# Second layer's modulation inside the first U stage, one-hots over fewer groups, and gathers shared out anew

## The chip, the cores and the metric

One core of a Trainium2 chip runs the whole program. The time is the device time of one execution in microseconds (us); the kernel before was timed in three runs. Engines: TensorE (PE, with its weight loads PEld), VectorE (DVE), ScalarE (ACT), GpSimd (POOL) and SyncE (SP), which here only issues DMAs. Each engine has one queue that it works off in order.

## The reference, cut to what matters

Two layers work on 512 latent and 256 context tokens of width 1024. Each layer begins with a modulation, six vectors of 1024 for the latent stream and six for the context:

```python
mod   = (silu_c  @ w_mod[l] + b_mod[l])[:, None, :]
mod_c =  silu_cc @ w_mod[l] + b_mod[l]
sh1, sc1, g1, sh2, sc2, g2 = jnp.split(mod, N_MOD, axis=-1)
h_lat = rms_norm(x_lat, norm_mix[l]) * (1.0 + sc1) + sh1
```

Then come a mixer (windowed attention A, neighbourhood attention B, an RWKV-7 scan C, an output projection) and PEER: a retrieval in which 8 heads pick 16 of 16384 experts for each token, by product keys.

```python
q = (hb @ wq).reshape(PEER_CHUNK, PEER_HEADS, 2, PEER_QDIM // 2)
s = jnp.einsum('thpd,hpnd->thpn', q, sub_keys).astype(jnp.float32)
sv, si = lax.top_k(s, PEER_TOPK)
...
gate = jax.nn.softmax(best, axis=-1)
ue = jnp.take(u, expert, axis=0)
ve = jnp.take(v, expert, axis=0)
act = jax.nn.gelu(jnp.einsum('td,thkd->thk', hb, ue).astype(jnp.float32), approximate=False)
return jnp.einsum('thk,thkd->td', (gate * act).astype(hb.dtype), ve)
```

The modulation of a layer does not depend on the tokens. In the second layer the context needs no PEER.

## The kernel before, in words

`run` goes through the two layers, each as `project` (norm and input projection), `mix` (scan, attention, output projection) and `peer`. Matrix products with float32 accuracy are three products of halves: each operand is split into H (a cast on ACT) and L (a subtraction, mostly on DVE), and `mm3` (L132) issues H·H, H·L and L·H.

**Modulation.** `mod_unit` (L151) computes one of six units of a layer: eight loads of 128 x 1024 weights (`wmod`, 512 KB each, on SP's queue, L164), 32 products in four column groups of PE (L161), four for the bias, a copy on ACT (L170), two stores to memory (`mscr`, ACT's queue), and for shift and scale two transposes and a copy to columns (L177 to L184). The first layer's six units run in its `project`. Of the second layer's, the first two (`NM1`) run between the softmaxes of the first layer's attention (`fill`, L577), the other four in the second layer's `project`, at a lower priority than the norms (L257).

**Attention.** `soft` (L581) takes one softmax of 128 rows: maximum on DVE, exponential on ACT, sum and reciprocal on DVE, a scaling of up to 640 columns on DVE (L603), transposes on PE, a copy on ACT. There are 48 in the first layer and 32 in the second.

**PEER, dense.** The dense tokens (512 in the first layer, 384 in the second) go against all experts. `scores` (L1103) makes 16 blocks of key scores (per block wH on ACT, wL on DVE at L1120, 24 matmuls, top-16 on DVE); it runs for the context, the first layer's latents and the second layer's. The U stage runs over 32 groups of four blocks of 128 experts: a U row of two blocks is loaded, split into uH and uL (L1311, L1313), multiplied (`pa`), put through Gelu on ACT (L1317) and stored. In between run the units of `gated`: for each of the four dense token tiles (three in the second layer) a choice of experts on DVE, then four units that build the gate matrix W of 32 tokens from one-hots (`oh`, `og` on DVE, small f16 matmuls `pw`, a copy on ACT into W, a store to `wscr`). `GSPREAD` says over how many groups these units are spread. When they are all issued, their memory is closed and a pool `ar2` opens in its place, in which the last `LATE` blocks of Gelu outputs stay instead of being stored; the first such block belongs to group 24 in the first layer. The V stage then runs over the groups: G = Gelu output times W, split, and multiplied with the split V rows into eight accumulators (`py`).

**PEER, gathered.** The remaining tokens (256 of the context in the first layer, 128 latents in the second) are done by gathers (`Gather`): one indirect DMA on POOL's queue fetches, for 128 tokens, one expert's row of 8 KB (U and V), DVE multiplies the U half with the token (L1464) and adds the weighted V half to `accc` (L1470); 256 gathers in the first layer, 128 in the second. They are issued by `tick`: `NTICK` has, per layer, how many gathers a tick is worth: in the scores, in the first `NFIRST` groups of U, in the rest of U, and in V. A tick comes every second block. What is left after V goes out in `flush`. Two gathers (`NQ`) are accumulated together.

**The ring.** All large weights of these stages and all gathers share one ring of six rows (`gat.row`, `NROW`), 8 KB in each partition, 1 MB a row. A row is filled anew when the last reader of its sixth predecessor is done, in the order of the program.

**The order.** The kernel is written with a framework that orders the instructions of each engine ahead of time, by a simulated timeline and priorities; the order on the chip is then fixed. `high_priority(offset=...)` moves work forward or, negative, back; gathers get the strongest push.

Of the kernel before, what the change touches and what calls it, by code (L numbers as in the profile page):

```python
# [8 lines left out]
F32 = mybir.dt.float32  # L9
# [5 lines left out]
OP = mybir.AluOpType  # L15
# [3 lines left out]
P = 128  # L19
# [16 lines left out]
NROW = 6  # L36
NQ = 2
MOFF = 500
GSPREAD = (24, 20)
LATE = (28, 28)  # L40
NM1 = 2
NMW = (6, 4)
NRAW = 4
TC0 = 6
NPSC, NPSL = 2, 4
# [9 lines left out]
NPRT = 4  # L55
NQKB = {"qs": 3, "kh": 3, "kl": 2}

NTICK = ((1, 1.0, 1.5, 2.4), (0, 0, 1.06, 1.06))
NFIRST = (12, 3)
FEATS = (12, 13, 4, 0, 5, 1, 6, 2, 7, 3, 14, 8, 9, 10, 11)  # L60
LAT = (0, 1, 2, 3)
# [5 lines left out]
class Kernel:  # L67
    nw = 0

    def __init__(self, ctx, tc, i, out, dbg):  # L70
        self.ctx, self.tc, self.nc, self.i, self.out, self.dbg = ctx, tc, tc.nc, i, out, dbg
        self.cp = ctx.enter_context(self.pool(name="cp", bufs=1))
        self.mods = list(range(NM1))

        self.xsb = {}
        self.consts()
        self.scratch()
# [70 lines left out]
        for ch in chunks:  # L148
            self.mod_unit(l, ch, pool, ps, "pm")

    def mod_unit(self, l, ch, pool, ps, tag):  # L151

        nc, i = self.nc, self.i
        c = slice(ch * 1024, ch * 1024 + 1024)
        src = i["w_mod"][l, :, c].rearrange("(k p) n -> p k n", p=P)
        b = pool.tile([P, 256], F32, name="bmod", bufs=1)
        nc.sync.dma_start(b[0::32], i["b_mod"][l, c].rearrange("(j m) -> j m", j=4))
        pm = ps.tile([P, 512], F32, name=tag)

        def add(j, lhs, rhs, first, last):  # L160
            nc.tensor.matmul(pm[32 * j:32 * j + 32, 0:256], lhs, rhs, start=first, stop=last)  # L161
        for k in range(KC):
            w = pool.tile([P, 1024], F32, name="wmod")
            nc.sync.dma_start(w, src[:, k])  # L164
            for j in range(4):
                add(j, self.cs[:, k], w[:, j * 256:j * 256 + 256], k == 0, False)
        for j in range(4):
            add(j, self.cs[32 * j:32 * j + 1, KC], b[32 * j:32 * j + 1], False, True)
        r = pool.tile([P, 256], F32, name="rmod", bufs=1)
        nc.scalar.copy(r, pm[:, 0:256])  # L170
        for z in range(2):
            nc.scalar.dma_start(self.mscr[l][z, c].rearrange("(j m) -> j m", j=4), r[z::32])
        which, part = divmod(ch, 3)
        if part < 2:
            pt = ps.tile([P, 512], F32, name=tag)
            for h in range(2):
                nc.tensor.transpose(pt[:, h * P:h * P + P], r[:, h * P:h * P + P], self.ident)  # L177
            m = self.mcol[:, l, which, :, part]
            nc.vector.tensor_copy(m.rearrange("p z (j h) -> p z j h", h=2),
                                  pt[:, 0:256].rearrange("p (h j m) -> p m j h", h=2, j=4)[:, 0:2])  # L180
            if part:
                o = (NMIX, NFFN)[which]
                for z in range(2):
                    nc.vector.scalar_tensor_tensor(m[:, z], m[:, z], 1.0, self.colp[l][:, o:o + 8], OP.add, OP.mult)  # L184
# [43 lines left out]
    def project(self, l, st):  # L228
# [3 lines left out]
        hp_ = st.enter_context(self.pool(name="hp", bufs=1))  # L232
        hH = hp_.tile([P, KC, T], F32R, name="hH")
        hL = hp_.tile([P, KC, T], F32R, name="hL")
        def mods(chunks):
            if s3.pools is None:
                s3.pools = [s3.enter_context(self.pool(name="mp", bufs=NMW[l], side="right")),
                            s3.enter_context(self.pool(name="mps", bufs=2, space=PSUM, side="right"))]
            self.mod(l, chunks, *s3.pools)

        def src(t):
            if l == 0:
                return i["x"][t * P:(t + 1) * P] if t < 4 else i["ctx"][(t - 4) * P:(t - 3) * P]
            return self.xp[t * P:(t + 1) * P]
        with ExitStack() as s3:
            s3.pools = None
            if l == 0:
                mods(range(2))
            with ExitStack() as s2:
                np_ = s2.enter_context(self.pool(name="np", bufs=2))  # L250
                nps = s2.enter_context(self.pool(name="nps", bufs=2, space=PSUM))
                mc = self.mcol[:, l, 0]
                for tiles in (CTX, LAT[:2], LAT[2:]):
                    self.norm_T(src, mc, hH, hL, tiles, np_, nps)
            if l:
                self.gat.close()
            with self.tc.high_priority(offset=-MOFF):  # L257
                mods(range(NM1 if l else 2, 6))
        ps = st.enter_context(self.pool(name="pps", bufs=2, space=PSUM))
        psn = st.enter_context(self.pool(name="psn", bufs=2, space=PSUM, side="right"))  # L260
        xp_ = st.enter_context(self.pool(name="xp", bufs=1, side="right"))
# [302 lines left out]
    def attention(self, l, st):  # L564
# [7 lines left out]
        nc.sync.dma_start(sink, i["a_sink"][l].partition_broadcast(P))  # L572
        am = ap.tile([P, 2, P], F32, name="am")
        nc.sync.dma_start(am, i["amask"])
        mp = st.enter_context(self.pool(name="mp", bufs=2))

        def fill():  # L577
            if self.mods:
                self.mod_unit(1, self.mods.pop(0), mp, psl, "pl")

        def soft(parts, h, use_sink):  # L581

# [17 lines left out]
                nc.vector.tensor_tensor(m[:, 3:4], m[:, 3:4], m[:, 5:6], OP.add)  # L600
            nc.vector.reciprocal(m[:, 3:4], m[:, 3:4])
            n = sum(n for _, n in parts)
            nc.vector.tensor_scalar(pr[:, :n], pr[:, :n], m[:, 3:4], None, OP.mult)  # L603
            prT = a2.tile([P, 640], F32, name="prT", bufs=NPRT)
            c = 0
            for pl, n in parts:
# [38 lines left out]
        def heads_A(tiles, lat):  # L645
            k0_ = 0 if lat else NLAT
            q0 = tiles[0] * P
            for e in range(2):
# [3 lines left out]
                for a, t in enumerate(tiles):  # L652
# [6 lines left out]
                    for z in range(2):  # L659
                        pl = psl.tile([P, 512], F32, name="pl")  # L660
                        parts = [(pl, nk + 256)] if nk <= 256 else [(pl, nk), (psl.tile([P, 512], F32, name="pl"), 256)]
                        pc, n = parts[-1]
                        q = qs[z][:, a * P:(a + 1) * P]
                        qk_mm(pc[:, n - 256:n], q, hd, lambda x: x[:, NLAT - k0_:])
                        if lat:
                            qk_mm(pl[:, 0:nk], q, hd, lambda x: x[:, k0 * P:(k1 + 1) * P])
                            if k0 < t:
                                nc.vector.tensor_tensor(pl[:, 0:P], pl[:, 0:P], am[:, 0], OP.add)
                            if k1 > t:
                                nc.vector.tensor_tensor(pl[:, nk - P:nk], pl[:, nk - P:nk], am[:, 1], OP.add)  # L670
                        fill()
                        prTs.append(soft(parts, 2 * e + z, True))
                    weigh(pl, prTs, [vals] * 2, o[:, a * P:(a + 1) * P])
                keep(e, o, q0)
# [30 lines left out]
        for c in range(2):  # L705
# [3 lines left out]
            for j in range(4):  # L709
                prTs = []  # L710
                for z in range(2):
# [9 lines left out]
                          lambda x: x[:, :NLAT].rearrange("p (r w) -> p r w", w=64)[:, :, reg[j]:reg[j] + 32])  # L721
                    qk_mm(pl[:, 256:512], qb, hd[z], lambda x: x[:, NLAT:])
                    nc.vector.tensor_tensor(pl[:, 0:256], pl[:, 0:256], bias, OP.add)
                    fill()
                    prTs.append(soft([(pl, 512)], h, False))
                weigh(pl, prTs, [[vb[:, j, y, h * 64:h * 64 + 64] for y in range(2)] +
                                 [vc[:, y, h * 64:h * 64 + 64] for y in range(2)] for h in (2 * c, 2 * c + 1)],
# [375 lines left out]
    def scores(self, l, hH, hL, tiles, sv, sif, st, tick=None, side=None):  # L1103
# [6 lines left out]
        for c in range(16):  # L1110
# [6 lines left out]
            wH = sp2.tile([P, KC, P], F32R, name="wH")  # L1117
            nc.scalar.copy(wH, wr)
            wL = sp2.tile([P, KC, P], F32R, name="wL")
            nc.vector.tensor_tensor(wL, wr, wH.bitcast(F32), OP.subtract)  # L1120
            n = len(tiles)
            pq = psq.tile([P, n * P], F32, name="pq")
            for k in range(KC):
# [142 lines left out]
    def peer(self, l, st):  # L1266
# [11 lines left out]
        with ExitStack() as sb:  # L1278
# [15 lines left out]
            it = self.places(sp)  # L1294
            up = sb.enter_context(self.pool(name="up", bufs=2))
            psu = sb.enter_context(self.pool(name="psu", bufs=2, space=PSUM))
            pw = sb.enter_context(self.pool(name="pw", bufs=2, space=PSUM))

            def scored(g, late=None):
# [33 lines left out]
            for g in range(32):  # L1333
# [3 lines left out]
                if done == 5 * len(dense) and units:  # L1337
                    units = None
                    sg.close()
                    late = sr.enter_context(self.pool(name="ar2", bufs=1, side="right"))  # L1340
                scored(g, late)
        with ExitStack() as sb:
            vp = sb.enter_context(self.pool(name="vp", bufs=2))
            psv = sb.enter_context(self.pool(name="psv", bufs=1, space=PSUM))
# [76 lines left out]
class Gather:  # L1421
# [26 lines left out]
    def row(self):  # L1448
        return self.gp.tile([P, 2 * D], F32, name="row", bufs=NROW)
# [104 lines left out]
```

## Time and profile before

| what | value |
|---|---|
| median of three runs | 5100.42 us (5089.33 to 5117.75) |
| profiled execution | 5089.21 us |
| its span, first to last instruction | 5087.4 us |
| busy: PE, DVE, ACT, POOL | 87%, 73%, 34%, 26% |
| mean granted clock of TensorE | 0.906 of full |
| moved by DMA | 1186.55 MB, mean 233 GB/s |
| first layer: U stage, V stage | 1122 to 2057 us, 2057 to 2860 us |
| second layer: from 2870 us; U stage, V stage | 3830 to 4510 us, 4510 to 5060 us |

A busy PE is one with matmuls in flight; their ends are modelled, so matmuls overlap in the rows. The times of the stages are read from the first and last instructions of their lines. What an engine waited for is inferred from semaphore events. An engine's idle time matters only where that engine's work ends last.

### The profile page before, as it was taken

How to read it: one execution, taken by the hardware profiler on the slowest of the kernel's cores; microseconds unless marked ns; L12 is line 12 of the kernel's file. 1: busy time of each engine (PE TensorE's matmuls, PEld its weight loads, DVE VectorE, ACT ScalarE, POOL GpSimd, SP SyncE). 2: the span in 40 equal slices, each digit the busy share in tenths (PEclk: the TensorE clock that was granted, in tenths of full speed). 3: DMA queues.
4: the chain of work that ended last, by engine and by line, in shares of the span. 5: the costliest groups of instructions: out<-in, count | busy, mean ns of one | idle time of the engine just before them, and what ended most of it. 6: DMA issues, size and time to landing. Idle time of an engine off the chain costs nothing. (4 is left out here: it accounts for less than half of the span.)

```text
span 5087.4 us, 74067 instructions
## 1 busy us (share of the span) xinstructions
PE 4438.3 (87%) x27525; PEld 3679.1 (72%) x27525; DVE 3738.1 (73%) x7611; ACT 1731.5 (34%) x2881; POOL 1338.2 (26%) x1403
## 2 busy tenths in 40 slices
PE   7778797689999979898889596799698998988999
PEld 4558666567888867787777364687578997977887
DVE  3964658869967754798888867758589877556887
ACT  3433234333333322222222244324333443332333
POOL 0536632011111111232222235455011111112121
PEclk9779887799999989999999787779799998999999
DMA  7434665235777755899999942573424887567998
GB/s 273 134 104 125 190 203 177 90 128 197 250 260 283 281 217 214 305 372 371 367 364 368 349 162 87 131 204 111 157 100 170 305 296 278 215 236 256 342 357 299
DMA packets 573865, 1186.55 MB, mean 233 GB/s; under 512 B 63152, under 2 KB 376384, under 8 KB 520768
## 3 DMA queue, kind: packets, MB, share of 16 engines
q1 hardware_dynamic: 507072, 758.39, 44.8%
q0 software_dynamic: 61440, 418.41, 22.1%
q10 hardware_dynamic: 4992, 5.02, 0.3%
q8 instruction: 216, 3.54, 0.3%
q14 instruction: 145, 1.19, 0.1%
HBM read 1005.19 MB, written 176.50 MB: 232 GB/s over the span
## 5 line engine op out<-in xcount | busy, mean ns | idle before, releaser
L1453 POOL DMA_INDIRECT row<-in_uv,eidx x384 | 580.2, 1511 | 2465.2 <-DVE accc L1470 1369.1
L136 PE MATMUL pa<-hH,uL 128*128 128x512 f32 (+1 forms) x2048 | 757.9, 370 | 36.0 <-DVE uL L1313 35.9
L134 PE MATMUL pa<-hH,uH 128*128 128x512 f32 (+1 forms) x2048 | 754.5, 368 | 25.8 <-ACT ar L1317 21.6
L135 PE MATMUL pa<-hL,uH 128*128 128x512 f32 (+1 forms) x2048 | 752.4, 367 | 0.0
L135 PE MATMUL py<-vL,GH 128*128 128x512 f32 x1792 | 705.9, 394 | 26.6 <-DVE vL L1365 26.5
L136 PE MATMUL py<-vH,GL 128*128 128x512 f32 x1792 | 698.4, 391 | 0.0
L134 PE MATMUL py<-vH,GH 128*128 128x512 f32 x1792 | 625.2, 397 | 67.5 <-ACT vH L1363 44.1
L1464 DVE SCALAR_TENSOR_TENSOR row<-row,h2c 128x1024 f32<-128x1024 f32 x384 | 467.6, 1220 | 293.6 <-DMA row<-in_uv,eidx 293.3
L1470 DVE SCALAR_TENSOR_TENSOR accc<-row,dt,accc 128x1024 f32<-128x1024 f32 x384 | 491.6, 1280 | 5.4
L1311 ACT CAST uH<-row 128x1024 fp32r<-128x1024 f32 x256 | 268.5, 1050 | 653.7 <-PE pa L135 582.2
L136 PEld LDWEIGHTS pa<-hH,uL 128*128 128x128 f32 x2048 | 391.4, 191 | 84.8 <-DVE uL L1313 45.8
L134 PEld LDWEIGHTS py<-vH,GH 128*128 128x128 f32 x1792 | 340.9, 191 | 148.6 <-ACT vH L1363 53.4
L134 PEld LDWEIGHTS pa<-hH,uH 128*128 128x128 f32 x2048 | 391.6, 191 | 66.6 <-ACT ar L1317 22.2
L135 PEld LDWEIGHTS pa<-hL,uH 128*128 128x128 f32 x2048 | 390.9, 191 | 39.4
L135 PEld LDWEIGHTS py<-vL,GH 128*128 128x128 f32 x1792 | 341.3, 190 | 105.6 <-DVE vL L1365 34.5
L1313 DVE TENSOR_TENSOR uL<-row,uH 128x1024 fp32r<-128x1024 f32 x256 | 311.8, 1220 | 128.4 <-ACT uH L1311 127.5
L136 PEld LDWEIGHTS py<-vH,GL 128*128 128x128 f32 x1792 | 339.6, 189 | 70.7
L1370 ACT CAST GH<-G 128x512 fp32r<-128x512 f32 (+1 forms) x256 | 145.0, 567 | 637.7 <-PE py L135 414.9
L1365 DVE TENSOR_TENSOR vL<-row,vH 128x1024 fp32r<-128x1024 f32 x256 | 309.4, 1218 | 26.5 <-ACT vH L1363 26.5
L1363 ACT CAST vH<-row 128x1024 fp32r<-128x1024 f32 x256 | 262.5, 1043 | 41.7 <-DMA row<-in_uv 23.1
L1239 PE MATMUL pw<-og,oh 128*128 128x128 f16 x1792 | 237.7, 297 | 33.5 <-DVE og L1234 23.5
L1231 DVE TENSOR_TENSOR oh<-iota,ix 128x512 f16<-128x512 f16 x448 | 170.5, 419 | 104.8 <-PE pw L1239 103.9
(385 smaller groups left out, 8577.1 us busy)
## 6 DMA issues: line engine op xcount, KB each, us to landing
row<-in_uT SPq DMA_DIRECT2D x128, 1024.0 KB
row<-in_uv SPq DMA_DIRECT2D x128, 1024.0 KB
wscr<-W SPq DMA_DIRECT2D x28, 2048.0 KB
wmod<-in_w_mod SPq DMA_DIRECT2D x96, 512.0 KB
wt<-wscr SPq DMA_DIRECT2D x32, 1024.0 KB
row<-in_wq SPq DMA_DIRECT2D x24, 1024.0 KB
ascr<-aw SPq DMA_DIRECT2D x96, 256.0 KB
av<-ascr SPq DMA_DIRECT2D x48, 512.0 KB
```

What stands on the lines that cost most here:

```text
L134: mm(out, lh, rh, start=first, stop=False)
L135: mm(out, lh, rl, start=False, stop=False)
L136: mm(out, ll, rh, start=False, stop=last)
L1231: nc.vector.tensor_tensor(oh[:, z], self.iota4, ix[:, z, tt].unsqueeze(1).to_broadcast([P, P, 4]), OP.is_equal)
L1239: nc.tensor.matmul(pw[:, q], oh[:, 1, :, q], og[:, z, :, q], start=z == 0, stop=z == 1)
L1311: nc.scalar.copy(uH, ur)
L1313: nc.vector.tensor_tensor(uL, ur, uH.bitcast(F32), OP.subtract)
L1363: nc.scalar.copy(vH, vr)
L1365: nc.vector.tensor_tensor(vL, vr, vH.bitcast(F32), OP.subtract)
L1453: self.K.nc.gpsimd.indirect_dma_start(out=r, out_offset=None, in_=self.K.i[f"uv{self.l}"], in_offset=bass.IndirectOffsetOnAxis(ap=self.idx ...
L1464: nc.vector.scalar_tensor_tensor(rows[z][:, 0:D], rows[z][:, 0:D], 1.0, self.h[:, a], OP.mult, OP.mult, accum_out=dt[:, z:z + 1])
L1470: nc.vector.scalar_tensor_tensor(acc, v, dt[:, z:z + 1], acc, OP.mult, OP.add)
```

## The change

Five things change, all in the order or the place of work; what is computed stays.

- All six units of the second layer's modulation run in the first layer's U stage, one after each of the groups 4, 9, 14, 19, 24 and 29. Their weights come through the ring, two slices of 512 KB to a row, four rows a unit. `fill` and the units in the second layer's `project` are gone, with their pools.
- `GSPREAD` goes from (24, 20) to (22, 18): the units of `gated` are spread over fewer groups.
- `NTICK` changes in both layers: more gathers in scores and U, fewer in V.
- `soft` scales on ACT.
- `scores` subtracts wL on POOL.

```diff
-GSPREAD = (24, 20)
+GSPREAD = (22, 18)
-NM1 = 2
-NMW = (6, 4)
-NTICK = ((1, 1.0, 1.5, 2.4), (0, 0, 1.06, 1.06))
+NTICK = ((2, 1.2, 2.0, 2.1), (0, 0, 1.2, 1.0))
...
-    def mod_unit(self, l, ch, pool, ps, tag):
+    def mod_unit(self, l, ch, pool, ps, tag, row=None):
...
-            w = pool.tile([P, 1024], F32, name="wmod")
-            nc.sync.dma_start(w, src[:, k])
+            if row is None:
+                w = pool.tile([P, 1024], F32, name="wmod")
+                nc.sync.dma_start(w, src[:, k])
+            else:
+                if k % 2 == 0:
+                    w2 = row().rearrange("p (k n) -> p k n", k=2)
+                    nc.sync.dma_start(w2, src[:, k:k + 2])
+                w = w2[:, k % 2]
...
-            if l == 0:
-                mods(range(2))
+            if wc:
+                mods = (s3.enter_context(self.pool(name="mp", bufs=6, side="right")),
+                        s3.enter_context(self.pool(name="mps", bufs=2, space=PSUM, side="right")))
+                self.mod(l, range(2), *mods)
...
-            with self.tc.high_priority(offset=-MOFF):
-                mods(range(NM1 if l else 2, 6))
+            if wc:
+                with self.tc.high_priority(offset=-MOFF):
+                    self.mod(l, range(2, 6), *mods)
...
-        def fill():
-            if self.mods:
-                self.mod_unit(1, self.mods.pop(0), mp, psl, "pl")
...
-            nc.vector.tensor_scalar(pr[:, :n], pr[:, :n], m[:, 3:4], None, OP.mult)
+            nc.scalar.activation(pr[:, :n], pr[:, :n], AF.Copy, scale=m[:, 3:4])
...
-            nc.vector.tensor_tensor(wL, wr, wH.bitcast(F32), OP.subtract)
+            nc.gpsimd.tensor_tensor(wL, wr, wH.bitcast(F32), OP.subtract)
...
+            if wc:
+                mu = (sb.enter_context(self.pool(name="mu", bufs=1)),
+                      sb.enter_context(self.pool(name="psm", bufs=1, space=PSUM)))
...
                 scored(g, late)
+                if wc and g % 5 == 4:
+                    self.mod_unit(1, g // 5, *mu, "pm", gat.row)
```

## Rows read from the trace of the kernel before

**Rows 1.** The page: busy time of the engines, and memory rate in 40 slices.

```profile
PE 4438.3 (87%) x27525; PEld 3679.1 (72%) x27525; DVE 3738.1 (73%) x7611; ACT 1731.5 (34%) x2881; POOL 1338.2 (26%) x1403
...
GB/s 273 134 104 125 190 203 177 90 128 197 250 260 283 281 217 214 305 372 371 367 364 368 349 162 87 131 204 111 157 100 170 305 296 278 215 236 256 342 357 299
```

**Rows 2.** Busy time in stretches: length; PE, PEld, DVE, ACT, POOL; clock; DMA share; GB/s.

```profile
860.00:1050.00 190.00, 147.37 (x881) 122.21 (x880) 144.85 (x598) 62.63 (x130) 9.74 (x32) 0.82 0.27 93
...
1122.00:2057.00 935.00, 888.18 (x4378) 730.71 (x4377) 682.30 (x1579) 309.88 (x473) 145.57 (x137) 0.97 0.66 240
2057.00:2860.00 803.00, 717.54 (x3072) 582.50 (x3072) 695.40 (x944) 215.37 (x335) 242.27 (x162) 0.97 0.99 362
```

**Rows 3.** The same in shorter stretches at the end of the U stage.

```profile
1790.00:1830.00 40.00, 40.00 (x208) 33.24 (x207) 27.64 (x45) 14.70 (x23) 5.30 (x4) 1.00 0.76 286
1830.00:1870.00 40.00, 16.33 (x119) 12.88 (x117) 26.38 (x51) 9.63 (x17) 4.57 (x3) 0.56 0.62 231
...
1877.00:2057.00 180.00, 168.71 (x716) 137.28 (x714) 84.50 (x98) 46.39 (x69) 31.44 (x21) 0.96 0.52 190
```

**Rows 4.** Timeline of PE and ACT there: start, length, instruction [idle before <- releaser].

```profile
1874.68 0.80 PE L134 MATMUL pa<-hH,uH 128*128 128x512 f32 x1 [14.04 <-ACT ar L1317]
...
1874.04 1.09 ACT L1317 ACTIVATE ar<-pa 128x512 f32<-128x512 f32 x2 [12.76 <-DMA wscr<-W]
```

**Rows 5.** V stage, first layer: busy time; PE's longest wait (total us, times, longest).

```profile
2057.00:2840.00 783.00, 717.54 (x3072) 582.50 (x3072) 676.62 (x918) 214.55 (x331) 230.19 (x155) 0.98 0.99 361
...
PE py L134 <- ACT vH L1363: 44.1, 22, 5.3
```

**Rows 6.** Timeline of PE: the first work after the V stage.

```profile
2884.94 1.08 PE L161 MATMUL pm<-wmod,cs 128*32 128x256 f32 x8 [46.29 <-DMA wmod<-in_w_mod]
```

**Rows 7.** Groups by line: count | busy us, mean ns | idle before, releasers.

```profile
L1470 DVE SCALAR_TENSOR_TENSOR accc<-row,dt,accc 128x1024 f32<-128x1024 f32 x384 | 491.6, 1280 | 5.4
L1464 DVE SCALAR_TENSOR_TENSOR row<-row,h2c 128x1024 f32<-128x1024 f32 x384 | 467.6, 1220 | 293.6 <-DMA row<-in_uv,eidx 293.3
```

**Rows 8.** Timeline of PE: two groups of a modulation unit back to back.

```profile
2900.65 0.64 PE L161 MATMUL pm<-wmod,cs 128*32 128x256 f32 x8
2901.22 0.63 PE L161 MATMUL pm<-bmod,cs 1*32 1x256 f32 x8
```

**Rows 9.** Stretches, line 161 alone: length, PE busy, PEld busy, clock, DMA share, GB/s.

```profile
620.00:700.00 80.00, 12.99 (x144) 3.22 (x144) 0.96 0.75 223
2860.00:2920.00 60.00, 13.04 (x128) 2.95 (x128) 0.61 0.93 337
2920.00:3020.00 100.00, 15.36 (x160) 4.30 (x160) 0.89 0.56 192
```

**Rows 10.** PE's waits in the second layer's U stage.

```profile
PE pa L134 <- ACT ar L1317: 7.5, 1, 7.5
```

**Rows 11.** Groups by line: scaling, exponential, wL on DVE, wL on POOL.

```profile
L594 ACT ACTIVATE pr<-pl,sm 128x512 f32<-128x512 f32 (+2 forms) x96 | 57.2, 599 | 63.7 <-DVE sm L590 58.8 <-PE pg L859 2.1 <-DVE sm L600 1.3
...
L1120 DVE TENSOR_TENSOR wL<-row,wH 128x1024 fp32r<-128x1024 f32 x48 | 58.2, 1218 | 24.2 <-ACT wH L1118 20.3 <-PE pS L1129 3.8
...
L603 DVE TENSOR_SCALAR pr<-pr,sm 128x512 f32<-128x512 f32 (+2 forms) x80 | 45.8, 577 | 1.1
...
L224 POOL TENSOR_TENSOR wL<-wr,wH 128x1024 fp32r<-128x1024 f32 x10 | 25.6, 2562 | 133.3 <-ACT wH L223 75.8 <-DMA wr<-in_w_in 54.4 <-issue 3.1
```

**Rows 12.** PE's waits from 720 to 1000 us.

```profile
PE pl L608 <- DVE pr L603: 28.5, 8, 13.8
```

**Rows 13.** Timeline of POOL and DVE in the second layer's norm.

```profile
2912.73 2.35 POOL L224 TENSOR_TENSOR wL<-wr,wH 128x1024 fp32r<-128x1024 f32 x1 [54.35 <-DMA wr<-in_w_in]
...
2911.26 0.29 DVE L216 CAST hH<-f 128x256 fp32r<-128x256 f32 x1 [1.74 <-ACT f L212]
...
2913.15 2.18 DVE L216 CAST hH<-f 128x256 fp32r<-128x256 f32 x1 [1.14 <-ACT f L212]
```

**Rows 14.** SP's waits in the first layer's U stage, for U rows.

```profile
SPq L1304 <- DVE uL L1313: 76.6, 16, 27.8
...
SPq L1304 <- DMA row<-in_uv,eidx: 46.0, 5, 16.1
```

More of the change, by code (lines that the diff above doesn't have):

```diff
@@ L72, in __init__ @@
         self.cp = ctx.enter_context(self.pool(name="cp", bufs=1))
-        self.mods = list(range(NM1))
         self.xsb = {}
@@ L234, in project @@
         hL = hp_.tile([P, KC, T], F32R, name="hL")
[L235 to L239, printed above, removed]
         def src(t):
@@ L245, in project @@
         with ExitStack() as s3:
-            s3.pools = None
-            if l == 0:
-                mods(range(2))
+            if wc:
+                mods = (s3.enter_context(self.pool(name="mp", bufs=6, side="right")),
+                        s3.enter_context(self.pool(name="mps", bufs=2, space=PSUM, side="right")))
+                self.mod(l, range(2), *mods)
             with ExitStack() as s2:
@@ L574, in attention @@
         nc.sync.dma_start(am, i["amask"])
-        mp = st.enter_context(self.pool(name="mp", bufs=2))
-        def fill():
-            if self.mods:
-                self.mod_unit(1, self.mods.pop(0), mp, psl, "pl")
         def soft(parts, h, use_sink):
@@ L670, in heads_A @@
                                 nc.vector.tensor_tensor(pl[:, nk - P:nk], pl[:, nk - P:nk], am[:, 1], OP.add)
-                        fill()
                         prTs.append(soft(parts, 2 * e + z, True))
@@ L723, in attention @@
                     nc.vector.tensor_tensor(pl[:, 0:256], pl[:, 0:256], bias, OP.add)
-                    fill()
                     prTs.append(soft([(pl, 512)], h, False))
```

## The prediction

> **What bounds the kernel now.** I read the page first, then the busy time stage by stage, then the waits inside the stages that the change touches. The page [rows 1] shows TensorE (PE) busy 87% of the span, and a memory rate that is uneven: about 280 GB/s in the middle of the span's first half, 360 to 370 GB/s in the slices around its middle. The stage table [rows 2] says which stages those are. The first layer's U stage (1122 to 2057 us) has PE busy 888 of 935 us with DMA at 0.66: PE sets its pace. The first layer's V stage (2057 to 2860) has DMA at 0.99, 362 GB/s, and PE busy 718 of 803: there memory, VectorE (DVE, 695) and PE stand close together, and PE waits. The stretch from attention's tail to the output projection (860 to 1050) has DVE 145 and PE 147 of 190, neither full, taking turns.
>
> Finer windows of the U stage [rows 3] show PE at 40 of 40 us shortly before its end, then 16 of 40 at 1830 to 1870, and 169 of 180 in the eight groups that are left. The hole is the hand-over of the one-hots' memory to late buffers; PE waits 14.0 us there in one piece for ACT, whose output tile waits for a store [rows 4]. In the V stage PE loses 65.5 us up to 2840 [rows 5], most of it waiting for vH, whose rows come late. After PE's last V matmul (it ends at 2838.6: the next one starts at 2884.9 after an idle of 46.3 [rows 6]) DVE still works off gathers that nothing covers.
>
> **The change part by part.** All sums are against the profiled execution, 5089.2 us (span 5087.4 and 1.8 around it); the median of the three runs, 5100.4, lies 0.2% above, and I don't correct for that.
>
> *Gathers.* From the code, the first layer issues 5 in the scores, 24 and 60 in U, 153.6 in V; 242 are out when V ends and 14 are left. After: 10, 28.8, 80 and 134.4; 253 are out, 3 left. So 30 move into scores and U, V loses 19 and the tail 11. One gather costs DVE 1.22 + 1.28 and a read of the accumulator, 2.6 us [rows 7], and memory 128 rows of 8 KB, 1.05 MB.
> - Tail: 11 x 2.6 = 28.6 us of DVE work with PE idle. Some lag of the last pair stays. I take -24, ends -15 and -28.
> - V stage: 19.2 gathers are 20.1 MB, at 362 GB/s 55.6 us of memory; the ceiling is PE's lost 65.5. DVE loses 50 of its 695 too. I take -45 because some of PE's stall is order, not volume; ends 0 and -65.
> - U stage: DVE gets 78 us more and is at 682 of 935 [rows 2], so PE hides it where the one-hots are spread. Memory: 240 GB/s x 935 = 224 MB, plus 31 MB for gathers and 25 MB for modulation, 280 MB, which at 362 GB/s is 774 us, below the stage. What remains is the ring of six rows, through which every weight and gather goes.
>
> *Modulation of the second layer.* A group of 8 matmuls (four column groups, two halves each) starts 0.57 us after the one before when its weights are there [rows 8]. A unit has 8 such groups and one for the bias: 5.1 us, with its transposes 5.5. Six units in a stage where PE is the bound: +33. What goes away: two units in the first layer's attention, 13.0 us of PE, and four at the start of the second layer, 13.0 and 15.4 us [rows 9], part of it at half clock (0.61). There the norms' transposes and the first features stand behind them on PE, and 16 MB of weights on SP's queue stand among w_in's loads. Not all is on the path: I take -12 for the second layer (ends -5, -28) and -8 for attention (ends 0, -13). Their stores on ACT's queue, two a unit, move along and cost nothing either way: ACT is busy 310 of 935 in U.
>
> *The rows of the modulation.* Each unit takes four rows of the ring, 24 in all, issued on SP in order; behind each stand U's weights and the stores of ACT's outputs. Before, the ring passed 64 weights and 84 gathers in U; now 64, 109 and 24. Where the one-hots are gone, the stage lost 11 us of PE at 2.5 rows a tick (180 less 169, [rows 3]); that stretch becomes three eighths longer (11 groups for 8) and has 3 to 3.4 rows a tick: 11 x 1.4 x 1.3 = 20, so 9 more. I double this for the bursts of four: +20. Ends: 0, and the second rival's price.
>
> *One-hots over 22 and 18 groups.* The same work, two groups earlier. The last unit's store has two groups (45 us at 180 for eight) to land before the first late buffer is written, so the 14.0 us of [rows 4] go, and the same wait of 7.5 us in the second layer [rows 10]. The remaining 14 us of that hole (PE waiting for og and for W's store, one-hots with no U work between them) may come back two groups earlier. I take -21; ends 0, -36.
>
> *Softmaxes on ScalarE, wL on POOL.* 80 scalings at 577 ns (46 us) leave DVE; on ACT the nearest row is its exponential over the same width, 599 ns [rows 11], so the chain of one softmax stays as long, and ACT has room (63 of 190 in [rows 2]). 48 subtractions at 1.22 us (58.5 us) leave DVE; on POOL the same shape took 2.56 [rows 11]. In the scores PE needs 24 matmuls a block, at 717.5 / 3072 = 0.234 us each [rows 5] 5.6 us for 512 tokens and half of it for 256; POOL is nearly empty there (10 of 190), so with two buffers 2.56 is hidden, barely for the context. What PE can win is what it waits for the scaled softmax: 28.5 us in the first layer's stretch [rows 12], as much in the second's. It waits because DVE is full of top-k work, of which only the wL and the scalings go: a third of both, -18. Ends: -57, and +57 as below.
>
> A row speaks against wL on POOL: while POOL subtracted (2912.7 to 2915.1), a cast on DVE that otherwise takes 0.29 us took 2.18 and ended with it [rows 13]. The Trainium skill's page "SBUF — State Buffer", section "Who interferes with whom", has the rule: DVE and GpSimd share a port pair, and one of them waits for the other's whole instruction when DVE casts or reads two SBUF operands. By that rule, this term would be a loss instead of -18. In the scores most DVE work is top-k over one operand, so by the row I keep -18; the gathers' multiplies and casts are where it would bite.
>
> *Second layer's ticks.* 8 gathers move from V to U; PE has slack in both. 0, ends -20 and +20.
>
> Sum: -24 - 45 + 33 - 12 - 8 + 20 - 21 - 18 = -75: **5014 us**.
>
> **The rivals.**
> 1. *Rows, not bytes, bound the V stage.* The wait that ends last before PE stalls is vH, after SP waited for a ring row; if a row's life is set by DVE's order, 3.1 rows a tick take as long as 3.4. For it: PE's stalls there are short and many. Against: DMA at 0.99. V keeps its time: 5014 + 45 = 5059.
> 2. *The modulation's rows block SP in U* (the other side). SP's wait for a U row was 76.6 / 16 = 4.8 us when a DVE use ended it and 46.0 / 5 = 9.2 when a gather's landing did [rows 14]. If each of the 24 rows adds such a wait in front of PE, the +20 becomes 115 or 221: 5109 or 5215. It decides from 5.5 us a row on: (5126 - 4994) / 24. For it: SP is in order, and a unit wants four rows at once. Against: PE stood at 40 of 40 in the gated part, so rows were in time.
> 3. *POOL and DVE shut each other out over wL.* Each of 48 wL then holds DVE up for about the 1.22 us that it saves, and 57 us are lost instead of 18 won: 5014 + 18 + 57 = 5089. For it: [rows 13]. Against: one-operand work dominates there. That POOL's queue has gathers waiting for rows ahead of a wL would have the same sign.
>
> **How the numbers follow.** The forecast has 0.70, with a range of its own from 4940 to 5070; rival 1 has 0.15, rival 2 has 0.08, rival 3 has 0.07. A measurement of this kernel can tell about 0.5% from no change, so faster means below 5075 and slower above 5126. The forecast counts as faster; rival 1, close to the bound, 0.09 as faster and 0.06 as the same; rival 3 as the same; rival 2 as slower. Faster 0.79, same 0.13, slower 0.08. The range: 4940 is the forecast with the V term at -65, the hand-over at -36 and half of the remaining favourable ends; 5095 takes in rivals 1 and 3 and leaves out rival 2 and the best ends together.
>
> **What would show it.** Right: the gap between PE's last V matmul and the next layer's first work falls from 46 us to about 20; V's DMA share falls below 0.97 and PE's busy share there rises above 0.94; no work on the second layer's modulation after the U stage; the U stage lasts 935 + 33 - 14 + 20, about 975 us; the 14 us wait of ar for W's store is gone; DVE in 860 to 1050 falls by some 25 us. Wrong: U above 1020 us with PE waiting for modulation rows (rival 2); V still 781 us with DMA below 0.95 (rival 1); wL's waits on PE above 20 us or max and cast on DVE stretched (rival 3).

## The result, and the profile after

The changed kernel took 5021.33 us (median of four runs, 5020.72 to 5022.01), the kernel before 5099.38 in the same comparison: a ratio of 0.9843, 95% interval 0.9815 to 0.9871. The forecast was 5014. The total was 7 us off, but several of its terms were wrong and cancelled, so the stages have to be looked at one by one. The profiled execution took 5020.74 us and its span is 5018.6; the stage lengths below, with 8.0 us from PE's last matmul to the end in both, add up to the spans.

Stages in us, from the first instruction of each stage to the first of the next (first layer unless said otherwise). A U stage begins here with the cast of its first weights, which in the second layer stands some 69 us ahead of the first product. In the first layer the products of the latent scores go on for some 50 us into the U stage, so these two are best read together. Each length comes from one profile. In later kernels whose changes lie elsewhere the same stretch differs by up to 10 us (the second layer up to U: 830.1 to 839.8), so less than that in one stage says little.

| stage | before | after | difference |
|---|---|---|---|
| start to scan | 521.3 | 521.8 | +0.5 |
| scan to context scores | 338.1 | 338.6 | +0.5 |
| context scores, rest of attention | 135.5 | 85.3 | -50.2 |
| output projection | 53.1 | 55.3 | +2.2 |
| norm and latent scores | 74.9 | 94.6 | +19.7 |
| U | 933.8 | 982.1 | +48.3 |
| V, to PE's last matmul | 782.0 | 744.5 | -37.5 |
| tail, to the first store | 39.2 | 9.5 | -29.7 |
| second layer, to its U stage | 863.3 | 830.1 | -33.2 |
| second layer, U and V | 1338.4 | 1348.9 | +10.5 |

First the page, the engines' busy time and the memory rate in 40 slices, which answer to [rows 1].

```profile
PE 4422.9 (88%) x27525; PEld 3666.1 (73%) x27525; DVE 3664.4 (73%) x7483; ACT 1770.7 (35%) x2957; POOL 1460.9 (29%) x1451
...
GB/s 274 138 105 118 180 160 165 119 200 189 282 294 321 315 323 223 298 346 370 367 370 364 237 117 100 142 193 104 173 85 229 313 302 259 235 268 257 322 346 251
```

PE has the same 27525 matmuls; the memory rate has risen in the slices of the U stage (321, 315, 323 for 283, 281, 217) and V is left shorter at the same plateau. Then the stretches that answer to [rows 2]: attention's tail with the output projection, U, and V (length; PE, PEld, DVE, ACT, POOL; clock; DMA share; GB/s).

```profile
860.00:1001.00 141.00, 126.05 (x780) 106.65 (x778) 111.54 (x509) 54.76 (x108) 45.49 (x48) 0.92 0.36 120
1095.00:2078.00 983.00, 927.47 (x4761) 740.06 (x4759) 721.81 (x1597) 307.38 (x483) 199.96 (x159) 0.98 0.75 276
2078.00:2822.00 744.00, 706.41 (x3072) 577.36 (x3072) 641.57 (x863) 212.81 (x323) 199.40 (x135) 0.99 1.00 358
```

In V DMA is at 1.00, so memory has no room left there. PE's busy share there is 706.41 / 744 = 0.95. In U, PE is busy 39 us longer than in [rows 2] and idle 9 us longer. The modulation's products alone in that stretch (line 158: PE, PEld, clock, DMA share, GB/s):

```profile
1095.00:2078.00 983.00, 36.06 (x432) 13.48 (x432) 0.98 0.75 276
```

The hand-over of the one-hots' memory, which answers to [rows 3]:

```profile
1840.00:1880.00 40.00, 24.91 (x191) 18.50 (x190) 22.20 (x39) 8.88 (x15) 6.71 (x5) 0.85 0.97 371
```

The hole is still there: PE 25 of 40 us. The timelines of ACT, DVE and PE show what ends it (they answer to [rows 4]).

```profile
1880.87 0.20 ACT L1463 ACTIVATE dt<-dt 128x2 f32<-128x2 f32 x1 [11.88 <-DVE row L1461]
1880.98 1.07 ACT L1312 ACTIVATE ar<-pa 128x512 f32<-128x512 f32 x2
```

```profile
1879.60 1.23 DVE L1461 SCALAR_TENSOR_TENSOR row<-row,h2c 128x1024 f32<-128x1024 f32 x1 [6.63 <-DMA row<-in_uv,eidx]
```

```profile
1881.61 0.80 PE L131 MATMUL pa<-hH,uH 128*128 128x512 f32 x1 [15.64 <-ACT ar L1312]
```

PE waits 15.6 us for the first Gelu into a late buffer, as before. This time ACT's last wait is put down not to the store of W but to a gather's dot product (dt, line 1463), which stands ahead of the Gelu on ACT's queue and whose product on DVE had itself waited 6.6 us for its row to land; the last store of W was issued at 1865.7, so it too may have held the Gelu for most of that time.

PE's waits in the V stage (total us, times, longest), which answer to [rows 5], and its first work after V, to [rows 6]:

```profile
PE py L131 <- ACT vH L1360: 20.5, 11, 3.6
PE py L131 <- ACT GH L1367: 15.2, 1, 15.2
```

```profile
2843.35 1.35 PE L213 MATMUL pt<-c_ident,xn 128*128 128x128 f32 x4 [21.16 <-DVE xn L207]
```

The wait for vH fell from 44.1 to 20.5 us, the gap after V from 46.3 to 21.2. What stays in V is one wait of 15.2 us for GH, the split of G, at the start of the stage (13.7 before).

### The profile page after: what moved, and what is told of

The parts are those of the page before. It is cut to its first block, busy times and chain, and to the rows that moved or that the text cites. A ratio compares the mean times of both kernels' runs of the same rounds, so it can differ in the third digit from the quotient of the medians.

```text
span 5018.6 us, 73997 instructions
## 1 busy us (share of the span) xinstructions
PE 4422.9 (88%) x27525; PEld 3666.1 (73%) x27525; DVE 3664.4 (73%) x7483; ACT 1770.7 (35%) x2957; POOL 1460.9 (29%) x1451
## 5 line engine op out<-in xcount | busy, mean ns | idle before, releaser
L1450 POOL DMA_INDIRECT row<-in_uv,eidx x384 | 593.0, 1544 | 2300.9 <-DVE accc L1467 1208.7
L1461 DVE SCALAR_TENSOR_TENSOR row<-row,h2c 128x1024 f32<-128x1024 f32 x384 | 472.6, 1233 | 280.5 <-DMA row<-in_uv,eidx 271.3
L1306 ACT CAST uH<-row 128x1024 fp32r<-128x1024 f32 x256 | 268.5, 1050 | 636.1 <-PE pa L132 547.1
L133 PEld LDWEIGHTS py<-vH,GL 128*128 128x128 f32 x1792 | 338.1, 189 | 70.0
```

The lines of the kernel that those rows point to most:

```text
L133: mm(out, ll, rh, start=False, stop=last)
L1306: nc.scalar.copy(uH, ur)
L1450: self.K.nc.gpsimd.indirect_dma_start(out=r, out_offset=None, in_=self.K.i[f"uv{self.l}"], in_offset=bass.IndirectOffsetOnAxis(ap=self.idx ...
L1461: nc.vector.scalar_tensor_tensor(rows[z][:, 0:D], rows[z][:, 0:D], 1.0, self.h[:, a], OP.mult, OP.mult, accum_out=dt[:, z:z + 1])
```

## The experiments

Each kernel was timed beside the kernel before on the same chip (5095 to 5101 us there). "Undo" kernels are the changed kernel with one part put back; "alone" kernels are the kernel before with one part of the change.

**1. Gathers: the old ticks in the changed kernel.**

```diff
-NTICK = ((2, 1.2, 2.0, 2.1), (0, 0, 1.2, 1.0))
+NTICK = ((1, 1.0, 1.5, 2.4), (0, 0, 1.06, 1.06))
```

> The changed kernel with the gathers shared out as before (1, 1.0, 1.5, 2.4 and 0, 0, 1.06, 1.06). Theory: the V stage is bound by bytes, so moving 30 gathers out of V and its tail is worth what V and tail lost (67 us) less what U pays for them (some 20): about 5065 to 5075. Tail gap back to about 39 us between PE's last V matmul and the first xp store, V about 780. Rival: gathers cost the same wherever they stand, V's gain comes back in U: within 10 us of 5021.

Measured 5076.53 us, ratio to before 0.9955 [0.9939, 0.9972]: the ticks are worth 55 us, the largest part of the change. V is 788.8 us instead of 744.5, the tail 39.2 instead of 9.5; the latent scores are 79.1 instead of 94.6, and U is 983.5 instead of 982.1. V in this kernel:

```profile
2070.00:2858.00 788.00, 724.48 (x3071) 587.38 (x3072) 683.35 (x925) 215.28 (x332) 239.67 (x156) 0.97 0.99 361
```

The rate is the same, 361 for 358 GB/s, and the stage 44 us longer: V shrinks with the bytes taken out of it, at the same rate, and the first rival, by which V keeps its time, falls. The 30 gathers moved into scores and U cost some 14 us there, 1076.7 us for the two stages together instead of 1062.6. How this splits between them is not shown, since they overlap: the changed kernel's score products (`pq`) still run when U's (`pa`) have begun, here between 1000 and 1300 us.

```profile
L131 PE MATMUL pq<-hH,wH x128: 387/389/792, 1026.4 to 1143.1; 128*128 128x512 f32 x128
```

```profile
L131 PE MATMUL pa<-hH,uH x196: 387/389/499, 1096.7 to 1299.4; 128*128 128x512 f32 x196
```

From the end of the output projection to the end of the score products both kernels take 143 us; with the old ticks U only begins earlier among them. The edit takes the second layer's ticks back too: its U and V take 1347.5 us then, and 1348.9 with the new ticks, no difference.

**2. Modulation: back in its old places (undo), and moved alone.** The undo restores `fill`, the second layer's units in `project` and the `wmod` tiles, as in the diff of the change read backwards; the other kernel makes that part of the change alone.

> The changed kernel with the second layer's modulation where it was (two units in attention, four in the second layer's projection). Theory of the forecast: the move costs 33 us of PE and 20 us of ring in U and wins 20 us in the mixers, so undoing it wins about 30: 4990. Rival, after the trace of the changed kernel, in which the two mixers together are 79 us shorter: the modulation blocks more in the mixers than its own PE time, so undoing it costs: mixers 40 to 60 us longer, U 45 shorter, total 5020 to 5040.

> The kernel before with the modulation moved and nothing else. Theory: the two units in attention hold attention up by some 40 us (its last products end 50 us earlier in the changed kernel), the four in the second layer's projection cost 25, and the first U stage pays 37: so the context scores to the first output projection shrink by 30 to 40 us, the second layer's features to scan by about 20, U grows by 30 to 40; total 20 to 30 below before, 5065 to 5080. Rival (the sum of the forecast): 33 us of PE and 20 of ring against 20 won: 30 above before.

Undone: 5036.46 us, 0.9888 [0.987, 0.9906], 15 slower than the changed kernel. Alone: 5055.64, 0.991 [0.9879, 0.9942], 42 faster than before. So the move wins, where the forecast's own terms (+33, +20, -12, -8) made it lose 33; the kernel with the move alone gained more than the expectation said (5065 to 5080). The U stage does pay: 950.9 us with the units in their old places, 982.1 with them inside, +31; alone it grows from 933.8 to 965.7, +32. But scan and attention of the first layer, from the first scan to the end of the output projection, take 517.1 us undone and 479.2 in the changed kernel (-38); alone the move takes them from 526.7 to 498.6 (-28). The second layer up to its U stage takes 839.3 undone and 830.1 in the changed kernel (-9); alone the move takes it from 863.3 to 823.8 (-40). The 9 us are within what this stretch varies by between profiles. To see why attention gains, count the softmaxes' first step, the maximum, that DVE has done between 600 and 700 us; first the changed kernel, then the undone one.

```profile
L579 DVE TENSOR_REDUCE sm<-pl 128x1 f32<-128x256 f32 (+1 forms) x18 | 7.8, 447 | 1.3 <-PE pl L637 1.1
```

```profile
L585 DVE TENSOR_REDUCE sm<-pl 128x1 f32<-128x256 f32 x2 | 0.8, 416 | 0.3 <-PE pl L643 0.3
```

With the units in attention, 2 of the 56 maxima are done by 700 us, without them 18. The kernel with the move alone has 14. In the undone kernel the `fill` units' products stand from 637 to 699 us, ahead of the softmaxes, while the scan's products run until 728; without the units attention runs beside the scan, and fewer of its softmaxes are left for the stretch behind it. What the units blocked, PE's fixed order or the memory of their pool, was not told apart.

**3. wL and the scaling, each back on DVE; the scaling alone.**

```diff
-            nc.gpsimd.tensor_tensor(wL, wr, wH.bitcast(F32), OP.subtract)
+            nc.vector.tensor_tensor(wL, wr, wH.bitcast(F32), OP.subtract)
```

> The changed kernel with wL back on VectorE. Theory: the context scores and the top-k beside attention are bound by DVE, POOL's 2.4 us are hidden, so undoing it costs about 10 us: 5031, all of it before the first output projection. Rival (port shut-out or POOL's queue): undoing it wins, above all in the first layer's scores, which became 20 us longer from the norm to the first U block: 5005 to 5015.

> The changed kernel with the softmaxes scaled on VectorE again. Theory: 80 scalings leave a full DVE where PE waits for them, so undoing it costs about 10 to 15 us, half in each mixer: 5031 to 5036. Rival: the chain of one softmax is what counts and is as long on either engine: within 3 us of 5021.

> The kernel before with the softmaxes scaled on ScalarE and nothing else. Theory: with the modulation still in attention the DVE is full beside it and the scaling is worth 10 to 25 us, most of it in the second layer's stretch from the first feature to the output projection (721 before); its value vanishes only once the modulation is gone. Rival (the chain of one softmax is as long on either engine): within 5 us of before in every stretch.

wL back on DVE: 5010.81 us, 0.9827 [0.9803, 0.9852], some 10 faster than the changed kernel: POOL is probably the wrong place. The intervals overlap, so this run by itself does not settle it; the later pair (experiment 6) has the same sign, 15 us, with intervals that overlap too but no run of one among those of the other. In the profiles norm, latent scores and U together take 1061.4 us instead of 1076.7, in the later pair 1026.2 instead of 1050.6, while the stretch behind the context's scores is 6.8 longer (92.1 for 85.3), in the later pair too (92.0 for 85.5): there POOL may be the right place. That mixture was not tried. Two larger differences of the first pair do not come again in the later one: the stretch up to the context's scores 10.3 longer, the second layer's U and V 9.7 shorter. The scaling back on DVE: 5019.59, 0.9845 [0.9828, 0.9861]; the scaling alone on ACT: 5090.91, 0.9989 [0.9974, 1.0003]. Both are no difference in the time. In the second profile the stages differ nevertheless: the second layer up to U is 16.2 us shorter (847.1 for 863.3), as the theory had it, V 9.5 and the stretch up to the context's scores 7.4 longer; whether these belong to the scaling is not shown.

What speaks for a loss by wL: POOL's and DVE's timelines in the changed kernel's latent scores, one subtraction, and two multiplies of the same shape, the first during it and the second with POOL free.

```profile
1066.28 2.39 POOL L1112 TENSOR_TENSOR wL<-row,wH 128x1024 fp32r<-128x1024 f32 x1
```

```profile
1067.24 2.51 DVE L1461 SCALAR_TENSOR_TENSOR row<-row,h2c 128x1024 f32<-128x1024 f32 x1 [0.61 <-DMA row<-in_uv,eidx]
...
1071.84 1.20 DVE L1461 SCALAR_TENSOR_TENSOR row<-row,h2c 128x1024 f32<-128x1024 f32 x1
```

POOL ends at 1068.67; the multiply that DVE had begun at 1067.24 ends 1.08 us later, about its own length of 1.20: it stood still until POOL was done. By the page "SBUF — State Buffer" of the Trainium skill, section "Who interferes with whom", a DVE instruction with two SBUF inputs contends with a GpSimd instruction that reads SBUF, and one with at most one SBUF input, outside the 2-port perf modes (in which it takes the shared port pair too), does not. The trace agrees on both counts: the multiply reads a row and h2c, while MAX8 over one operand, a good part of the scores' work, keeps its pace (the 115 in the scores that overlap a wL average 280 ns, the other 205 278). One input alone is no safeguard: the cast of [rows 13] has one and was held. The groups of the whole run, the multiply and wL:

```profile
L1461 DVE SCALAR_TENSOR_TENSOR row<-row,h2c 128x1024 f32<-128x1024 f32 x384 | 472.6, 1233 | 280.5 <-DMA row<-in_uv,eidx 271.3 <-issue 4.6 <-PE pw L1231 3.5
...
L1112 POOL TENSOR_TENSOR wL<-row,wH 128x1024 fp32r<-128x1024 f32 x48 | 117.3, 2449 | 207.6 <-ACT wH L1110 176.6 <-DMA kt<-in_keysT 31.0
```

Over the 384 multiplies the mean rises from the 1220 ns of [rows 7] to 1233, 5 us in all: few multiplies run beside a wL. Other two-operand instructions are held too. Taken together, the DVE instructions that overlap a wL last some 19 us longer than the median of their kind, 14 of them between 1000 and 1300 us, where the latent scores are; 16 instructions account for it. POOL needs 2449 ns for one subtraction, twice DVE's 1218 [rows 11], but PE waits little for it, 2.5 us in the whole run:

```profile
PE pq L133 <- POOL wL L1112: 2.5, 4, 1.0
```

So what holds DVE up is of the size of the loss and lies where the loss is; that it causes the loss is not shown, since DVE also loses 58 us of work, and what wL's place in POOL's queue does to the gathers there was not tried.

Why the scaling wins nothing: groups by line with different shapes kept apart, first the scaling and the exponential on ACT in the changed kernel, then the scaling on DVE in the kernel before; last PE's wait for the scaling from 680 to 946 us, which answers to [rows 12].

```profile
L597 ACT ACTIVATE pr<-pr,sm 128x512 f32<-128x512 f32 x48 | 33.6, 722 | 14.2 <-DVE sm L595 11.2 <-DVE sm L594 2.3 <-DVE sm L584 0.5
L588 ACT ACTIVATE pr<-pl,sm 128x512 f32<-128x512 f32 x48 | 32.8, 686 | 17.5 <-DVE sm L584 17.3
```

```profile
L603 DVE TENSOR_SCALAR pr<-pr,sm 128x512 f32<-128x512 f32 x48 | 29.3, 612 | 0.6
```

```profile
PE pl L602 <- ACT pr L597: 31.4, 3, 23.6
```

Over 128 x 512 one takes 722 ns on ACT where DVE took 612, ACT waits for DVE's sums ahead of it, and PE's wait is 31.4 us where it was 28.5. The chain of a softmax is no shorter than it was.

**4. The hand-over: the old spread (undo), and fewer late blocks.**

```diff
-GSPREAD = (22, 18)
+GSPREAD = (24, 20)
```

> The changed kernel with the one-hots over 24 and 20 groups again. Forecast's theory: the hand-over to the late buffers costs 14 and 7 us more: 5042. Rival, after the trace of the changed kernel, in which the hole at the hand-over is still there (15.6 us in one wait): the spread only shifts it, within 5 us of 5021, and U is as long.

```diff
-LATE = (28, 28)
+LATE = (20, 28)
```

> The changed kernel with 20 late blocks instead of 28 in the first layer, so that the first late buffer is wanted at group 26 and not 24. Theory: the hole at the hand-over is the wait for the last W store and goes when two groups lie between them: the 15.6 us wait in U is gone, U 15 us shorter, V some 2 MB longer (8 blocks stored and read back, 4 MB, 11 us at 358 GB/s): total 5 us below to 5 us above 5021. Rival: the order puts the last one-hots wherever the first late block stands, and the hole moves with it: U as long, V longer: 5025 to 5035.

The old spread: 5024.63 us, 0.9852 [0.9821, 0.9884], no difference; the 22 and 18 groups do nothing. The one-hots' products show it, in the kernel before, the changed one and the one with the old spread (count, ns, first and last start):

```profile
L1239 PE MATMUL pw<-og,oh x512: 278/297/302, 1602.5 to 1860.3; 128*128 128x128 f16 x171
```

```profile
L1231 PE MATMUL pw<-og,oh x464: 275/297/303, 1605.0 to 1864.2; 128*128 128x128 f16 x155
```

```profile
L1231 PE MATMUL pw<-og,oh x480: 275/297/303, 1603.8 to 1870.0; 128*128 128x128 f16 x160
```

In the changed kernel and the one with the old spread, the last stands at 1864 and 1870 us, 6 us apart, and U itself begins 6.7 us later in the second, where the two groups between the spreads are 61 (a 32nd of 982 us each): here the group at which the program issues a unit does not set when it runs. U's groups go ahead of it until the first late buffer stops them, so the hole lies where the U work that needs no late buffer ends. The second kernel moves that point two groups back, and it fills the hole, here in the 40 us with the hole in them:

```profile
1840.00:1880.00 40.00, 39.43 (x257) 30.52 (x256) 23.36 (x39) 12.45 (x20) 7.40 (x5) 1.00 0.94 356
```

5001.84 us, 0.9807 [0.9778, 0.9837]: 20 faster than the changed kernel, more than either expectation. U falls from 982.1 to 956.0 and V rises from 744.5 to 747.9 only; the last one-hot product stands at 1869 us, so the hole did not move with the first late block.

**5. The modulation's ring rows.** One row for a unit instead of four; the unit's other products use the first row's slices again, so three quarters of the second layer's modulation weights are left out.

```diff
-                if k % 2 == 0:
+                if k == 0:
```

> The changed kernel with one ring row per unit of the second layer's modulation instead of four: three quarters of the modulation's weights (18 of 24 rows, 18.9 MB) are left out, and the products use the first two slices again, so PE has the same work. The forecast put +20 us on the 24 rows of the ring and +33 on PE. If the rows cost that, the U stage falls from 982 us to about 967 and the run to 5006. The theory after the runs so far is that the stage's growth (934 to 982, of which PE's busy time grew by 39.5) is PE's work alone: U stays at 980 to 985 and the run at 5018 to 5024.

Measured 5012.63 us, 0.9831 [0.9814, 0.9847]. U is 952.3 us, 30 less, so the theory that the growth of U was PE's work alone fell: the rows cost time there, as the forecast's term had it. SP's waits for U's rows in the changed kernel had this one:

```profile
SPq L1299 <- PE pm L158: 63.0, 8, 25.2
```

In the kernel with one row little of it is left:

```profile
SPq L1299 <- PE pm L158: 3.2, 2, 2.8
```

So SP hardly waits any more for a modulation product to give a row back. This is the second rival's mechanism in a mild form. Two things bound the reading. With the rows their 18.9 MB are left out, and the two were not told apart; and 8 of the 30 us are the wait at the hand-over, which is 7.7 us here instead of 15.6. The whole run gained only 9 us, because V took back 11 (755.5 for 744.5) and two stretches in which nothing was changed another 11 (6 ahead of U, 5 ahead of the second layer's U). Why V is longer stays open; its rate was 350 GB/s for 358.

**6. The two finds together, then in the second layer too, then further.** wL on DVE with LATE = (20, 28), (20, 20) and (12, 12).

> The changed kernel with 20 late blocks in the first layer instead of 28 and wL back on DVE. The two alone measured -20 and -10 us. If they lie in different stages and add up, 4991 us. If the second only shifts work that the first one's filled hole already hides, 5001, as with late blocks alone. U stage 950 to 958 us, no wait of PE for ar above 5 us in it.

> As the version with 20 late blocks in the first layer and wL on DVE, with 20 late blocks in the second layer too. The second layer's U stage has one wait of PE for ar of 13.9 us in the changed kernel. If this hole is the same hand-over as in the first layer, it goes: 8 to 16 us less than with the first layer's alone, 4975 to 4983. If the V stage pays it back (8 more blocks are stored and loaded, 2.1 MB twice), no difference: 4991.

> As the version with 20 late blocks in both layers and wL on DVE (4946.75 us), with 12 late blocks in both. If the late blocks' only price is the hand-over hole, that hole is gone already and nothing is left to win: 4940 to 4952. If each block that is stored and loaded again costs the memory-bound V stage its 0.26 MB twice, 8 blocks in the first layer are 2.1 MB more to load, at 358 GB/s 6 us, and as much to store in U where memory has room: 4953 to 4960, the first layer's V stage 750 instead of 744 us.

(20, 28): 4987.2 us, 0.9779 [0.9763, 0.9795]; the two add up (15 us less than late blocks alone). (20, 20): **4946.75 us, 0.9698 [0.9681, 0.9715]**, faster than both kernels and the fastest of the study; 40 us below (20, 28), where 8 to 16 were expected. (12, 12): 4974.28, 0.9749 [0.9732, 0.9765], above both expected ranges.

The second layer's hole with 28 late blocks, PE's timeline, and then the stretch around it in the two kernels, 28 first:

```profile
4223.73 0.69 PE L131 MATMUL pa<-hH,uH 128*128 128x384 f32 x1 [13.96 <-ACT ar L1312]
```

```profile
4200.00:4300.00 100.00, 80.92 (x451) 78.92 (x451) 47.16 (x59) 28.92 (x46) 10.56 (x9) 0.84 0.55 200
```

```profile
4200.00:4300.00 100.00, 94.65 (x553) 92.18 (x552) 61.54 (x79) 35.03 (x57) 17.96 (x13) 1.00 0.74 278
```

PE gains 13.7 us in that stretch, about the wait itself, and the granted clock is 1.00 (2.4 GHz throughout) instead of 0.84 (partly 1.2 GHz). The second layer's U stage is 38 us shorter (754.0 for 792.1), more than twice the 14 us wait. Part of that lies ahead of the hole: from 3700 to 4200 us PE is busy for 475.5 us instead of 462.4. PE's other pauses and the clock's fall went with the hole; how much each is worth was not tried separately. With 12 blocks the first layer's U stays at 944.0 us and V goes from 743.7 to 756.6; the hole was gone already, and V, to which the bytes of 8 blocks return, is 13 us longer, where 6 were expected. The second layer's U loses 13 of its gain too. Of the numbers tried, 28, 20 and 12, 20 is the best.

## Why the prediction was right, and where it was not

The total came out (5014 forecast, 5021 measured, inside the likeliest case's own range), by the gathers' terms for V and the tail, which were right, and by misses of both signs around them.

- **Gathers, tail and V (-24, -45): right.** Measured -29.7 and, by the undone ticks, -44.3. The step that carried it, bytes at the stage's rate, gave 55.6; the runs bear out the 45 that the forecast made of it, but not the reason it gave, the order of PE's work, which was not tried. One sign was wrong: DMA's share in V did not fall below 0.97, it rose to 1.00. The stage remains bound by memory at the lower volume.
- **Gathers moved into the scores and U (0): too low.** The forecast held that PE hides them and gave them no price; the two stages together are some 14 us longer by them.
- **Modulation in U (+33) with its rows (+20): right in kind, too high in sum.** The two were 53 together and measured 31. PE's part is 36.06 us of products; the rows with their bytes are worth up to 30 by themselves. The two don't add up to the growth; why is not shown.
- **Modulation out of attention (-8): the step that failed.** It priced the two units by PE's 13.0 us [rows 9]. They cost what stood behind them: 38 us of scan and attention in the changed kernel, 28 alone. The second layer's start (-12) measured -9 in the changed kernel, not clear of what profiles vary by, and -40 alone. This turned a forecast loss of 33 for the whole move into a gain of 15, or of 42 alone. The two differ by 27, hardly more than their margins, so it stays open whether the parts of the change add up.
- **One-hots over fewer groups (-21): the second step that failed.** It measured nothing. The step took the units' place in the program for their time on the chip. The sign named for it, the 14 us wait gone, was absent: 15.6; the same wait in the second layer is 13.9 us where it was 7.5 [rows 10].
- **wL and scaling (-18): the third.** The scaling is nothing; its nearest row, 599 ns, was a mean over three shapes, and the exponential over 512 columns takes 686. wL is probably a loss of 10 to 15. The third rival had the sign; its mechanism is there, but its price of 57 (48 times 1.22 is 58.5) was far too high: not every wL holds DVE up, 16 DVE instructions did the most of it, some 19 us in all. By the rule of the Trainium skill's page named above the term was a loss; the measurement, as far as it goes, sides with that sign.
- **Second layer's ticks (0): right.** Undone, they change its U and V by 1.4 us. What makes the two 10.5 us longer than before stays open; it is little more than they vary by between profiles.

The sums, by the table: scan, attention and the second layer up to U -80 us where -38 was forecast (-8, -12, -18); latent scores and U +68 where +39 was (33 + 20 - 14; undone one at a time, the gathers, the modulation and wL take 14, 37 and 15 of it back); V and tail -67 where -69 was; the second layer's U and V +10.5 where -7 was. The errors, -42, +29, +2 and +17.5, leave 6 of the 7 us. That the total came so close is luck.

Of the signs: the gap after V (21.2 for 20), U (982 for 975) and PE's share in V (0.95, above 0.94) came as said. No work on the second layer's modulation is left after the U stage. DVE in 860 to 1050 us did not fall: it is 151.0 us in that window, where [rows 2] have 144.9, since the next stage now begins in it. Over attention's tail and the output projection alone, which end at 1001, it is 111.5, but part of that fall is softmaxes that ran earlier.

## What to carry to other kernels

Price work that is taken out of a chain by what was queued behind it, not by its own busy time: two units of 6.5 us held attention back by some 30 us. Where a framework orders the instructions, look up in the trace when an instruction ran before pricing a change of its place in the program; the point where its neighbours run out of work (here the first late buffer) is the better handle. In the stage with DMA at 0.99, moving 20 MB to stages with room gave back 44 us, four fifths of their time at the stage's own rate.

## What the runs showed that was not expected

- With a hole of 14 us on PE filled, the second layer's U stage was 38 us shorter, part of it ahead of the hole; the granted clock around the hole went from 0.84 to 1.00.
- The same two-operand multiply on DVE took 1.20 us alone and 2.51 us beside a POOL subtraction, which itself took 2.39 us.
- Over 128 x 512 elements the scaling takes ACT 722 ns and the exponential, which also sums, 686 ns; the accumulator's read behind the exponential is a row of its own (197 ns, 96 times).
